# Less GpSimd work at the second norm, a sample step in full tiles, and another instruction order in a two-layer decoder step

## The chip, the cores and the metric

The kernel runs on one core of a Trainium2 chip. The metric is the device time of one execution in microseconds (us), as the median of several runs. The engines are named as the profile names them: PE is TensorE (matmuls), PEld its weight loads, DVE is VectorE, ACT is ScalarE, POOL is GpSimd, and SP (SyncE) issues most of the DMAs. "PEclk" in the profile is the granted clock of TensorE as a share of full speed.

## The reference

The program is one inference step of a hybrid decoder with two layers. There are T = 1032 token columns: 1024 of a prompt and 8 of a sample, one new token for each of 8 sequences with 8192 cached positions. Each layer computes:

```python
h = rmsnorm(x, g_norm1) * (1 + scale1) + shift1
proj = h @ w_in                                   # z, xbc, dt, cq, ckv, kpe, u
ssd  = ssd_mixer(...)       # Mamba-2: 6 heads x 64, state 128, 2 groups; prompt by chunks,
                            # sample by one step from state_ssm
mla  = attend(...)          # latent attention; the sample reads 64 pages of 128 positions a sequence
pool = pool_mixer(...)      # trailing means
mix  = concatenate([ssd, mla, pool]) @ w_out
x  = x + gate1 * mix
h2 = rmsnorm(x, g_norm2) * (1 + scale2) + shift2
x  = x + gate2 * ((silu(h2 @ w_gate) * (h2 @ w_up)) @ w_down)
```

The step of the sample in the SSD mixer is, for each sequence b and head h, state = exp(dt a) state + B (dt x)^T, then y = C . state + D x.

## The kernel before, in words

Columns are tokens, partitions are features. A product of fp32 values is made of three matmuls: every operand is cut into a high part (an ACT copy to fp32r, L88) and a low part (a subtraction, L89, on DVE or POOL as a constant says), and `mm3` (L133 to L135) issues high x high, low x high, high x low. The token columns of the FFN and of the output projection are cut into four quarters of 258 columns; a half `g` holds two.

A layer goes through these stages (in layer 0, us of the span): the input projection (to about 310); the **weave** (about 320 to 1030), in which `Weave` advances three generators in turn: `sample` (the pages of the sample's attention; `L1140`, `L1141` cut a page, L133 to L135 with 390 columns make its keys, L1158 and L1305 their norms, and 32 softmax steps a layer follow), the chain `ssd_prompt`, `ssd_sample`, `ssd_finish`, `mla_prompt`, and blocks of the next adaLN table; then the output projection `out_proj` (about 1030 to 1122, half 0 then half 1, eight rows `m` of output each); the second norm with the first FFN passes (1122 to about 1200); the other FFN passes; and the down projection. Layer 1 repeats it some 1800 us later.

One softmax step of `sample` is: L1190 makes `md` (DVE); L1195 multiplies it (one small matmul into `psm`); DVE subtracts at L1196; ACT takes the exponential at L1199 (`pb`); PE multiplies `pb` with the pages at L1205 (16 matmuls of 129 columns).

`ssd_sample` makes, for each of two groups g and two quarters q of the sequences, a new state `h` of 128 x 768 values: an outer product (L665, 8 partitions deep), a decay and an addition. `product` (L637 to L641) then multiplies it with C: 8 matmuls in pairs, each with a state tile as the weights (128 or 64 columns of it) and one moving column of C.

The second norm: `out_proj` makes the residual (L1411), its squares (ACT, L1417) and adds them over m (L1423, DVE for odd m, POOL for even m); `norm_half` sums over partitions by a matmul with ones (L1447), makes the reciprocal root `r` (L94 to L103), multiplies (`fresh`: L1457, then the scale on DVE, L1462, for k in `XFV` and on ACT, L1465, otherwise; L1469 and L1470 for the sample's columns) and builds the seven operands X of a Strassen product: `sub` (L1481) forms a sum, `cut` splits it into high and low, with POOL for the low part if the operand is in `XPL`. FFN pass n takes one of 22 blocks of columns of the weights through seven products (`PO`); the first two blocks are done for half 0 alone (passes 0 and 1), then for half 1 alone (passes 2 and 3), the other twenty for both. `up_conv` prepares the weights of a product: sums at L1538 (POOL if in `WPS` for the first blocks) and a cut (POOL if in `WPF`); `up_load` loads a block by two DMAs on SP. `up_first` loads the first block and prepares WAH = 3 products ahead. The FFN adds partial products at L1578 and multiplies gate and up at L1624.

The order of the instructions on each engine is not written out: a scheduler takes the program in its order as priority and decides by a simulation of the program which instruction comes next. Tiles of 128 x 1032 come from a pool of 24 buffers ("a") and of 128 x 1548 from one of 20 ("b").

Of the kernel before, what the change touches and what calls it, by code (L numbers as in the profile page):

```python
# [10 lines left out]
ALU = mybir.AluOpType  # L11
# [37 lines left out]
class Net:  # L49
# [385 lines left out]
    def softplus(self, l):  # L435
# [159 lines left out]
    def ssd_sample(self, l):  # L595
        nc, A = self.nc, self.A
        acr, ea = self.acr, self.ea
        x = [self.pj[6 + i] for i in range(3)]
        Bf = [self.pj[9 + i] for i in range(2)]
        Cf = [self.pj[11 + i] for i in range(2)]  # L600

        p = self.Gp()
        for h in range(6):
            nc.tensor.matmul(p[:, NB * h:NB * h + NB], self.K(K_ID + h, 1, r1=6).to_broadcast([6, 128]), ea,
                             start=True, stop=True)
        px = self.Gp()
        for i in range(3):
            for e in range(2):
                nc.tensor.matmul(px[64 * e:64 * e + 64, NB * i:NB * i + NB],
                                 self.K(K_ID + 64 + 2 * i + e, 1, 64, 70).to_broadcast([6, 64]), acr[64:70, TP:],  # L610
                                 start=True, stop=True)
        eb = self.S([128, 6, NB], "eb", bufs=1)
        nc.vector.tensor_copy(eb, p[:, 0:48].rearrange("p (h b) -> p h b", h=6))
        xd = self.S([128, 3, NB], "xd", bufs=1)
        for i in range(3):
            nc.vector.tensor_tensor(out=xd[:, i, :], in0=x[i][:, TP:], in1=px[:, NB * i:NB * i + NB],
                                    op=ALU.mult)
        yield 3
        p = self.Gp()
        for i in range(3):  # L620
            nc.tensor.transpose(p[0:NB, 128 * i:128 * i + 128], xd[:, i, :], self.K(K_ID, 128))
        xn = self.C(name="xnb")[0:NB, 0:384]
        nc.vector.tensor_copy(xn, p[0:NB, 0:384])
        p = self.Gp()
        for g in range(2):
            nc.tensor.transpose(p[0:NB, 128 * g:128 * g + 128], Bf[g][:, TP:], self.K(K_ID, 128))
        bn = self.C(name="bnb")[0:NB, 0:256]
        nc.vector.tensor_copy(bn, p[0:NB, 0:256])
        yield 3
        ysb = self.S([128, 24], "ysb", bufs=1)  # L630
        def product(g, q, h1):
            yp = self.Gp()
            for b in range(4):
                o = 192 * b
                cc = Cf[g][:, TP + 4 * q + b:TP + 4 * q + b + 1]
                if g == 0:
                    nc.tensor.matmul(yp[:, b:b + 1], h1[:, o:o + 128], cc, start=True, stop=True)  # L637
                    nc.tensor.matmul(yp[0:64, 4 + b:5 + b], h1[:, o + 128:o + 192], cc, start=True, stop=True)
                else:
                    nc.tensor.matmul(yp[64:128, b:b + 1], h1[:, o:o + 64], cc, start=True, stop=True)  # L640
                    nc.tensor.matmul(yp[:, 4 + b:5 + b], h1[:, o + 64:o + 192], cc, start=True, stop=True)  # L641
            for j, r, a in (((0, slice(0, 128), 0), (1, slice(0, 64), 4)) if g == 0 else
                            ((1, slice(64, 128), 0), (2, slice(0, 128), 4))):
                nc.vector.tensor_copy(ysb[r, 8 * j + 4 * q:8 * j + 4 * q + 4], yp[r, a:a + 4])

        pend = None
        def state(i):
            g, q = divmod(i, 2)
            h0[i] = self.C(name="h0")
            nc.sync.dma_start(h0[i][:, 0:768], A["sssm"][l, :, g, 4 * q:4 * q + 4, :].rearrange("n b e -> n (b e)"))  # L650
        h0 = {}
        state(0)
        for g in range(2):
            for q in range(2):

# [3 lines left out]
                nc.vector.tensor_tensor(  # L659
                    out=rhs[0:NB, 0:768].rearrange("p (b e) -> p b e", b=4),  # L660
                    in0=xn[:, 192 * g:192 * g + 192].unsqueeze(1).to_broadcast([NB, 4, 192]),
                    in1=self.K(K_ID + 4 * q, 4, r1=NB).unsqueeze(2).to_broadcast([NB, 4, 192]), op=ALU.mult)
                d = [self.Gp() for _ in range(2)]
                for a in range(2):
                    nc.tensor.matmul(d[a][:, 0:384], bn[:, 128 * g:128 * g + 128], rhs[0:NB, 384 * a:384 * a + 384],  # L665
                                     start=True, stop=True)
                for b in range(4):
                    (nc.gpsimd if PH else nc.vector).tensor_tensor(
                        out=h1[:, 192 * b:192 * b + 192].rearrange("p (h e) -> p h e", h=3),
                        in0=h0[2 * g + q][:, 192 * b:192 * b + 192].rearrange("p (h e) -> p h e", h=3),  # L670
                        in1=eb[:, 3 * g:3 * g + 3, 4 * q + b].unsqueeze(2).to_broadcast([128, 3, 64]), op=ALU.mult)
                del h0[2 * g + q]
                for a in range(2):
                    e = slice(384 * a, 384 * a + 384)
                    nc.vector.tensor_tensor(out=h1[:, e], in0=h1[:, e], in1=d[a][:, 0:384], op=ALU.add)
                nc.sync.dma_start(A["o_sssm"][l, :, g, 4 * q:4 * q + 4, :].rearrange("n b e -> n (b e)"), h1[:, 0:768])
                if pend is not None:
                    yield W_H
                    product(*pend)
                pend = g, q, h1  # L680
                yield
        yield 4
        product(*pend)
        yield
        for j in range(3):
            nc.vector.scalar_tensor_tensor(out=self.y[j][:, TP:], in0=x[j][:, TP:], scalar=self.V(l, V_DSK + j),
                                           in1=ysb[:, 8 * j:8 * j + 8], op0=ALU.mult, op1=ALU.add)

    def ssd_finish(self, l):
        nc = self.nc  # L690
# [680 lines left out]
    def out_proj(self, l, mod, xsrc, side):  # L1371
# [6 lines left out]
        for i, (g, m) in enumerate(todo):  # L1378
# [181 lines left out]
    def up_first(self, l):  # L1560

        self.passes = [(f, (g,)) for g in range(2) for f in range(NG0)] + [(f, (0, 1)) for f in range(NG0, FF)]
        self.wraw, self.wtmp, self.wop = {}, {}, {}
        self.nx = 0
        self.up_load(l, 0)
        for j in range(WAH):
            self.up_conv(l, j)

    def ffn(self, l, X, mod, side, sink):

# [9 lines left out]
        done = WAH + WA0  # L1580
        for j in range(7 * len(self.passes)):
            while done <= j + WAH:
                self.up_conv(l, done)
                done += 1
            n, i = divmod(j, 7)
            f, gs = self.passes[n]
            if j >= SD0 or gs != (0,):
# [119 lines left out]
def build(nc, tc, A):  # L1707
    with tc.tile_pool(name="c", bufs=1) as cp, tc.tile_pool(name="s", bufs=1) as sm, \
# [54 lines left out]
        for l in range(L):  # L1763
# [46 lines left out]
            for j in range(WA0):  # L1810
                n.up_conv(l, WAH + j)
            side = n.norm_half(1, mod, gs, 3, X)
            for _ in range(SD1):
                next(side)
# [170 lines left out]
def program(nc, arrays):  # L1985
# [25 lines left out]
```

## Time and profile before

| | before |
|---|---|
| median of 3 runs | 3662.61 us (3662.19 to 3663.1) |
| the profiled execution's own time | 3663.35 us |
| its span, first to last instruction | 3661.6 us |
| mean granted TensorE clock | 0.962 |
| busy in the span: PE, DVE | 3436.4 us, 2358.1 us |
| busy in the span: ACT, POOL | 1732.6 us, 1546.8 us |

The profiled execution is a run of its own beside the three; its time is 1.75 us above its span. Stages are given in us from the start of the span. A busy PE does not say that it works at full speed: PEclk has to be read with it.

### The profile page before, as it was taken

Reading aid. Unit: us, or ns where it says so; the run is one execution under the profiler, and the core shown is the slowest. Engines: PE = TensorE matmul, PEld = TensorE weight load, DVE = VectorE, ACT = ScalarE, POOL = GpSimd, SP = SyncE. Lnnn points to the kernel's source line nnn. Section 1 sums busy time; section 2 is a strip of 40 time slices with the busy share of each in tenths; the row PEclk is TensorE's granted clock in tenths of the full one; section 3 lists DMA queues with packets and bytes.
Section 4 is the critical chain, followed back from the end, with each engine's and each line's share of the span. In section 5 each row is a group of like instructions: output and inputs, shape, how many; then the busy total and the mean of one; then the engine's idle time right before and its main releaser. Section 6 shows DMA issues by size and latency. Waiting matters only on the chain. (4 is left out here: it accounts for less than half of the span.)

```text
span 3661.6 us, 66619 instructions
## 1 busy us (share of the span) xinstructions
PE 3436.4 (94%) x23740; PEld 3091.1 (84%) x23740; DVE 2358.1 (64%) x4308; ACT 1732.6 (47%) x4455; POOL 1546.8 (42%) x1173
## 2 busy tenths in 40 slices
PE   8988989899997999999999899998998979999999
PEld 6977767677787999999999776677777979999999
DVE  4568686778878555542345687777877685555433
ACT  4227466777844333331132365777776443333220
POOL 2225444444244655543222254445453455555431
PEclk9999799999998999999999998999999989999999
DMA  5234555544442222142222255554443522222432
GB/s 199 47 83 146 167 180 174 157 139 117 142 143 86 86 80 86 72 173 89 81 77 61 81 168 174 176 149 112 125 126 109 159 79 82 77 81 81 170 97 70
DMA packets 255322, 430.10 MB, mean 117 GB/s; under 512 B 38736, under 2 KB 180944, under 8 KB 254992
## 3 DMA queue, kind: packets, MB, share of 16 engines
q1 hardware_dynamic: 246800, 409.04, 35.2%
q0 software_dynamic: 8192, 16.79, 1.8%
q8 instruction: 190, 3.11, 0.4%
q14 instruction: 140, 1.15, 0.1%
HBM read 372.84 MB, written 52.87 MB: 116 GB/s over the span
## 5 line engine op out<-in xcount | busy, mean ns | idle before, releaser
L1158 ACT ACTIVATE sqk<-psd 128x384 f32<-128x384 f32 x1024 | 497.6, 503 | 234.2 <-PE psd L135 184.5
L1141 POOL TENSOR_TENSOR lt<-pg,lt 128x512 fp32r<-128x512 f32 x256 | 311.3, 1224 | 544.1 <-ACT lt L1140 426.5
L1305 DVE TENSOR_REDUCE ss<-sqk 128x12 f32<-128x768 f32 x448 | 421.3, 943 | 127.0 <-ACT sqk L1158 125.7
L133 PE MATMUL psd<-mv,lt 128*128 128x390 f32 x1024 | 439.8, 429 | 7.0 <-ACT scr L1159 6.9
L134 PE MATMUL psd<-X,wp 128*128 128x258 f32 x1408 | 400.9, 285 | 3.2 <-DVE wp L89 3.2
L133 PE MATMUL psd<-X,wp 128*128 128x258 f32 x1408 | 401.2, 285 | 0.0
L135 PE MATMUL psd<-X,wp 128*128 128x258 f32 x1408 | 400.8, 285 | 0.0
L134 PE MATMUL psd<-mv,lt 128*128 128x390 f32 x1024 | 369.6, 361 | 5.9 <-POOL lt L1141 5.9
L135 PE MATMUL psd<-mv,lt 128*128 128x390 f32 x1024 | 367.8, 359 | 0.0
L134 PE MATMUL psg<-X,wp 128*128 128x258 f32 x1056 | 302.9, 287 | 35.4 <-DVE wp L89 35.4
L135 PE MATMUL psg<-X,wp 128*128 128x258 f32 x1056 | 302.2, 286 | 0.0
L133 PE MATMUL psg<-X,wp 128*128 128x258 f32 x1056 | 301.8, 286 | 0.0
L1093 POOL DMA_INDIRECT kp<-kpeT,kidx x256 | 249.1, 973 | 124.2 <-issue 91.6
L133 PEld LDWEIGHTS psd<-mv,lt 128*128 128x128 f32 x1024 | 204.4, 200 | 105.4 <-issue 46.4
L89 POOL TENSOR_TENSOR wl<-wr,wh 128x1024 fp32r<-128x1024 f32 x47 | 125.7, 2679 | 374.5 <-ACT wh L88 288.3
L134 PEld LDWEIGHTS psd<-X,wp 128*128 128x128 f32 x1408 | 269.5, 191 | 3.5 <-DVE wp L89 3.5
L133 PEld LDWEIGHTS psd<-X,wp 128*128 128x128 f32 x1408 | 269.9, 192 | 0.0
L133 PE MATMUL psd<-op,wh 128*128 128x348 f32 (+1 forms) x792 | 252.6, 319 | 18.1 <-DVE pb L419 9.5
L135 PEld LDWEIGHTS psd<-X,wp 128*128 128x128 f32 x1408 | 269.6, 191 | 0.0
L134 PE MATMUL psd<-op,wl 128*128 128x348 f32 (+1 forms) x792 | 251.0, 317 | 10.5 <-DVE wl L89 5.7
L135 PE MATMUL psd<-op,wh 128*128 128x348 f32 (+1 forms) x792 | 249.8, 317 | 1.8 <-POOL op L89 1.4
L89 POOL TENSOR_TENSOR wp<-wr,wp 128x512 fp32r<-128x512 f32 x128 | 167.1, 1306 | 198.5 <-ACT wp L88 194.0
(466 smaller groups left out, 9898.6 us busy)
## 6 DMA issues: line engine op xcount, KB each, us to landing
pg<-pages SPq DMA_DIRECT2D x1024, 129.0 KB
wa<-wada SPq DMA_DIRECT2D x96, 512.0 KB
wr<-wff SPq DMA_DIRECT2D x96, 512.0 KB
ar<-actd SPq DMA_DIRECT2D x44, 516.0 KB
actd<-G SPq DMA_DIRECT2D x40, 516.0 KB
wd<-wdn SPq DMA_DIRECT2D x48, 384.0 KB
wr<-win SPq DMA_DIRECT2D x32, 512.0 KB
wr<-wout SPq DMA_DIRECT2D x32, 512.0 KB
```

The source lines that it names most:

```text
L89: (eng or nc.gpsimd).tensor_tensor(out=l, in0=x, in1=h.bitcast(F32), op=ALU.subtract)
L133: nc.tensor.matmul(ps, wh, xh, start=start, stop=False)
L134: nc.tensor.matmul(ps, wl, xh, start=False, stop=False)
L135: nc.tensor.matmul(ps, wh, xl, start=False, stop=stop)
L1093: self.nc.gpsimd.indirect_dma_start(out=kts[-1][:, 128 * g:128 * g + 128], out_offset=None, in_=self.A["kpeT"], in_offset=bass.IndirectOff ...
L1141: nc.gpsimd.tensor_tensor(out=ll, in0=v, in1=lh.bitcast(F32), op=ALU.subtract)
L1158: nc.scalar.activation(out=sq, in_=d[:, kc], func=AF.Square)
L1305: nc.vector.tensor_reduce(out=o, in_=x, axis=AX.X, op=ALU.add)
```

## The change

It has three parts. (1) `TileContext` is opened with `schedule_with_timeline_sim=True`, so that the scheduler decides by its timeline simulation. (2) In `ssd_sample`, tiles of 6 or 8 partitions are now tiles of 128 with zeros around the values; `product` now takes a tile `zc` (C of eight sequences, one column every 129, zeros elsewhere) as the weights and the state as 192 moving columns: four matmuls that add up into one bank, where row b of the result is sequence b; three transposes at the end turn the result back. (3) Around the second norm the constants `XPL`, `XFV`, `WPF`, `WPS` are emptied: the low parts of X and of the first weights and the first weights' sums go from POOL to DVE, and the scale of k = 1, 3 from DVE to ACT. `OPV` names the weights of `out_proj` whose low part DVE makes: 9, 11, 13, 15 are added. The sum of squares of half 1 is all on DVE. `up_first` goes from after half 0 of `out_proj` to its row m = 3, and two weights each are prepared at m = 4 to 7, so that eight are ready ahead where three were.

```diff
--- before.py
+++ after.py
...
-        ea = self.ea = self.S([6, NB], "ea", bufs=1)
-        nc.scalar.activation(out=ea, in_=p[0:6, 128 - NB:128], func=AF.Exp)
+        ea = self.ea = self.S([128, NB], "ea", bufs=1)
+        nc.gpsimd.memset(ea, 0.0)
+        nc.scalar.activation(out=ea[0:6], in_=p[0:6, 128 - NB:128], func=AF.Exp)
...
+        t = self.C(name="xnb")
+        xn, bn, xd = t[:, 0:384], t[:, 384:640], t[:, 640:1024].rearrange("p (i x) -> p i x", i=3)
+        nc.gpsimd.memset(xd, 0.0)
...
+        zs = [self.C(name="zc") for _ in range(2)]
+        for z, cf in zip(zs, Cf):
+            nc.gpsimd.memset(z, 0.0)
+            nc.vector.tensor_copy(z[:, 0:129 * NB].rearrange("p (b x) -> p b x", x=129)[:, :, 0], cf[:, TP:])
         yield 3
...
         def product(g, q, h1):
             yp = self.Gp()
-            for b in range(4):
-                o = 192 * b
-                cc = Cf[g][:, TP + 4 * q + b:TP + 4 * q + b + 1]
-                if g == 0:
-                    nc.tensor.matmul(yp[:, b:b + 1], h1[:, o:o + 128], cc, start=True, stop=True)
-                    nc.tensor.matmul(yp[0:64, 4 + b:5 + b], h1[:, o + 128:o + 192], cc, start=True, stop=True)
...
-                nc.vector.tensor_copy(ysb[r, 8 * j + 4 * q:8 * j + 4 * q + 4], yp[r, a:a + 4])
+            for b in range(4 * q, 4 * q + 4):
+                o = 192 * (b - 4 * q)
+                nc.tensor.matmul(yp[:, 0:192], zs[g][:, 128 * b:128 * b + 128], h1[:, o:o + 192], start=b == 4 * q,
+                                 stop=b == 4 * q + 3)
...
                 for a in range(2):
-                    nc.tensor.matmul(d[a][:, 0:384], bn[:, 128 * g:128 * g + 128], rhs[0:NB, 384 * a:384 * a + 384],
+                    nc.tensor.matmul(d[a][:, 0:384], bn[:, 128 * g:128 * g + 128], rhs[:, 384 * a:384 * a + 384],
                                      start=True, stop=True)
...
+        p = self.Gp()
+        for j in range(3):
+            nc.tensor.transpose(p[:, 128 * j:128 * j + 128], yb[:, 128 * j:128 * j + 128], self.K(K_ID, 128))
...
                 for _ in range(SDO):
                     next(side[0], None)
+            elif m == UF0:
+                self.up_first(l)
+            elif m > UF0:
+                for _ in range(UFN):
+                    self.up_ahead(l)
...
-                (nc.vector if m % 2 else nc.gpsimd).tensor_tensor(out=sqs[z], in0=sqs[z], in1=sq, op=ALU.add)
+                (nc.vector if g or m % 2 else nc.gpsimd).tensor_tensor(out=sqs[z], in0=sqs[z], in1=sq, op=ALU.add)
...
-        for j in range(WAH):
-            self.up_conv(l, j)
+        self.done = 0
+
+    def up_ahead(self, l):
+        self.up_conv(l, self.done)
+        self.done += 1
...
-            n.up_first(l)
             side[0] = n.norm_half(0, mod, gs, 3, X)
...
-WPT, WPL, XPT, XPL, GUP = (0, 1, 2, 3), (0, 2, 4, 6), (), (1, 5, 7), 0
+WPT, WPL, XPT, XPL, GUP = (0, 1, 2, 3), (0, 2, 4, 6), (), (), 0
...
+UF0, UFN = 3, 2
 WA0, W_L, W_F, W_G = 0, 10, 28, 5
 OPO = (6, 7, 0, 1, 2, 3, 4, 5)
-XFV, WPF, WPS, OPV = (1, 3), (2,), (0, 1), (0, 2, 4, 6, 8, 10, 12, 14)
+XFV, WPF, WPS, OPV = (), (), (), (0, 2, 4, 6, 8, 9, 10, 11, 12, 13, 14, 15)
...
-    with tile.TileContext(nc) as tc:
+    with tile.TileContext(nc, schedule_with_timeline_sim=True) as tc:
```

In the order of PE's instructions, the first fences show a softmax step of layer 0 (names: `md` is what L1190 made, `pb` the exponentials, `psm` the bank; L1195 of before is L1204 of after, L1205 is L1214). Before:

```order
L1195 MATMUL psm_2986<-md_2923,kt 128x6
L135 MATMUL psd_2992<-mv_1410,lt_2886 128x390
L133 MATMUL psd_3009<-mv_1410,lt_2886 128x390
L134 MATMUL psd_3009<-mv_1410,lt_2886 128x390
L510 MATMUL psg_2975<-acr_1626,kt 128x128 x3
L510 MATMUL psg_2998<-acr_1626,kt 128x128 x3
L135 MATMUL psd_3009<-mv_1410,lt_2886 128x390
...
L573 MATMUL psg_3055<-M_2802,xn_2961 64x128
L575 MATMUL psg_3055<-E_2803,st_2251 64x128
L1205 MATMUL psm_3068<-pg_2211,pb_190 32x129 x4
```

After:

```order
L1204 MATMUL psm_2987<-md_2924,kt 128x6
L544 MATMUL psg_3153<-cv_1738,cv_1391 128x128
L544 MATMUL psg_3153<-cv_1877,cv_1573 128x128
L556 MATMUL psg_3166<-kt,cv_1027 128x128
L556 MATMUL psg_3166<-kt,cv_1128 128x128
L556 MATMUL psg_3166<-kt,cv_1229 128x128
L1214 MATMUL psm_3069<-pg_2212,pb_190 32x129 x4
```

Before, 21 rows of other work (seven matmuls of 390 columns and 18 of 128) stand between the small matmul and the one that needs its exponentials; after, five matmuls of 128 columns do. Over the 64 steps of the program the columns between the two have a median of 4530 before and of 2720 after. For L828 to L853 of `mla_prompt` it is the other way, 12,700 and 22,400.

The next fences show PE in `ssd_sample` of layer 0 (`h` is a state, `cv` holds C, `hr` is the outer product's right side, `psg_3916` and `psg_3924` are the product's banks). Before:

```order
L665 MATMUL psg_3874<-hr_3868,bnb_3781 128x384
L637 MATMUL psg_3916<-cv_1737,h_579_3838 128x1
L638 MATMUL psg_3916<-cv_1737,h_579_3838 64x1
L133 MATMUL psd_3990<-mv_1410,lt_3858 128x390
L134 MATMUL psd_3990<-mv_1410,lt_3858 128x390
```

After:

```order
L671 MATMUL psg_3882<-hr_3876,xnb_3715 128x384
L133 MATMUL psd_4004<-mv_1410,lt_3866 128x390
L134 MATMUL psd_4004<-mv_1410,lt_3866 128x390
L135 MATMUL psd_4004<-mv_1410,lt_3866 128x390
L642 MATMUL psg_3924<-h_578_3846,zc_3723 128x192 x4
```

The pair L637, L638 stands four times before (once shown); in its place four matmuls of 192 columns follow each other. One such group stands in each layer for each g and q.

The last fences show DVE in the second norm of half 1 in layer 0 (`xb` is the residual, `r` the reciprocal root, `wp` a prepared weight, `G` and `s` FFN sums; L1457 of before is L1471 of after, L1578 is L1595). Before:

```order
L103 SCALAR_TENSOR_TENSOR r_13551<-rw_13553,r_13551 128x258
L1457 TENSOR_TENSOR xb_12941<-xb_12941,r_13551 128x1032
L1457 TENSOR_TENSOR xb_12942<-xb_12942,r_13551 128x1032
L1462 TENSOR_SCALAR xb_12941<-xb_12941,gs_12918,mod_76 128x258 x2
L1462 TENSOR_SCALAR xb_12942<-xb_12942,gs_12918,mod_76 128x250 x2
L1469 TENSOR_TENSOR xb_12942<-xb_12942,gs_12918 128x4x8
L89 TENSOR_TENSOR wp_13603<-wt_12925,wp_13603 128x512
```

After:

```order
L103 SCALAR_TENSOR_TENSOR r_13565<-rw_13567,r_13565 128x258
L1595 TENSOR_TENSOR s_13615<-s_13615,psg_13673 128x258
L1595 TENSOR_TENSOR G_13613<-G_13613,psg_13658 128x258
L1471 TENSOR_TENSOR xb_12956<-xb_12956,r_13565 128x1032
L1471 TENSOR_TENSOR xb_12954<-xb_12954,r_13565 128x1032
L89 TENSOR_TENSOR wp_13688<-wr_12741,wp_13688 128x512
```

Before, the first weight `wp` that DVE cuts in this place stands behind the whole normalization; after, FFN sums (L1595) stand between its parts, since eight weights are already prepared, and no L1462 is left on DVE. From the first L94 of half 1 to the fourth L1639 (L1624 of before) DVE's order of after holds 36 instructions of 258 columns, 30 of 512, 15 of 1032, 4 of 516 and 6 small ones. On SP, the four loads of the first two FFN blocks (`wr` from `wff`) stand between the sixth and the ninth load of `out_proj`'s weights; before, the first pair stood behind the tenth and the second pair behind the last of them.

## Rows read from the trace of the kernel before

**Rows 1.** The page: the span, and busy time of each engine.

```profile
span 3661.6 us, 66619 instructions
PE 3436.4 (94%) x23740; PEld 3091.1 (84%) x23740; DVE 2358.1 (64%) x4308; ACT 1732.6 (47%) x4455; POOL 1546.8 (42%) x1173
```

**Rows 2.** Windows: length, busy time of each engine, PEclk, DMA share, GB/s.

```profile
core 0: us, PE busy (x) PEld busy (x) DVE busy (x) ACT busy (x) POOL busy (x), PEclk, DMA share, GB/s
372.00:432.00 60.00, 58.07 (x299) 44.88 (x298) 33.59 (x76) 22.55 (x74) 25.16 (x31) 0.72 0.61 194
432.00:1020.00 588.00, 541.29 (x3486) 423.44 (x3485) 461.45 (x846) 423.84 (x1332) 257.66 (x232) 0.96 0.49 146
1030.00:1080.00 50.00, 49.65 (x402) 48.90 (x402) 31.84 (x48) 20.17 (x38) 19.61 (x12) 1.00 0.52 170
1080.00:1120.00 40.00, 35.78 (x271) 35.37 (x272) 35.62 (x46) 18.48 (x31) 20.82 (x9) 0.91 0.46 145
1120.00:1190.00 70.00, 50.65 (x341) 49.40 (x340) 64.56 (x92) 35.45 (x65) 27.70 (x14) 0.80 0.23 76
2186.00:2254.00 68.00, 64.57 (x344) 50.42 (x342) 41.68 (x97) 27.74 (x94) 27.04 (x33) 0.77 0.56 181
2254.00:2820.00 566.00, 522.73 (x3371) 413.90 (x3371) 448.59 (x821) 417.93 (x1313) 255.16 (x228) 0.96 0.47 136
2920.00:2990.00 70.00, 50.74 (x342) 49.48 (x342) 62.81 (x89) 34.74 (x62) 27.92 (x15) 0.80 0.23 78
```

**Rows 3.** Waits of PE: who ended them, us in total, times, longest.

```profile
PE psg L134 <- DVE wp L89: 35.4, 7, 8.6
PE psg L853 <- DVE rx L839: 12.2, 4, 3.2
PE psm L1205 <- ACT pb L1199: 11.7, 7, 3.2
PE psm L1195 <- DVE md L1190: 11.3, 12, 2.5
```

**Rows 4.** A fine window of PE in the sample's step: busy, PEclk, DMA share, GB/s.

```profile
398.00:402.00 4.00, 4.00 (x10) 0.50 0.00 0
```

**Rows 5.** PE's timeline in layer 0: start, us, instruction.

```profile
334.81 0.81 PE L583 MATMUL psg<-xn 128*128 128x192 f32 x4
...
411.86 0.28 PE L640 MATMUL psg<-cv,h 128*64 128x1 f32 x2
...
412.38 0.28 PE L640 MATMUL psg<-cv,h 128*64 128x1 f32 x2
```

**Rows 6.** One softmax step on the timelines of PE and ACT.

```profile
327.66 0.28 PE L1195 MATMUL psm<-md,kt 128*128 128x6 f32 x2
```
```profile
331.26 0.32 ACT L1199 ACTIVATE pb<-scr 128x96 f32<-128x96 f32 x1
```

**Rows 7.** PE's timeline at the second norm of half 1, layer 0.

```profile
1122.06 0.59 PE L1447 MATMUL psd<-sq,kt 128*128 128x258 f32 x2
...
1137.96 0.58 PE L134 MATMUL psg<-X,wp 128*128 128x258 f32 x1 [8.60 <-DVE wp L89]
```

**Rows 8.** DVE's timeline at the same place, and the end of pass 3.

```profile
1131.82 5.38 DVE L1462 TENSOR_SCALAR xb<-xb,gs,mod 128x258 f32<-128x258 f32 x4
...
1140.01 1.22 DVE L89 TENSOR_TENSOR X<-xb,X 128x1032 fp32r<-128x1032 f32 x1
...
1142.36 0.41 DVE L1578 TENSOR_TENSOR G<-G,psg 128x258 f32<-128x258 f32 x1
1142.69 0.68 DVE L89 TENSOR_TENSOR wp<-wr,wp 128x512 fp32r<-128x512 f32 x1
1143.30 0.41 DVE L1578 TENSOR_TENSOR s<-s,psg 128x258 f32<-128x258 f32 x1
...
1195.68 1.35 DVE L1624 TENSOR_TENSOR G<-G,U 128x516 f32<-128x516 f32 x1 [0.41 <-ACT G L1623]
```

**Rows 9.** POOL: its timeline beside rows 8, and its memsets of 1032 columns.

```profile
1130.50 3.62 POOL L89 TENSOR_TENSOR X<-xb,X 128x1032 fp32r<-128x1032 f32 x1 [11.37 <-ACT X L88]
```
```profile
L471 POOL MEMSET acr<- 128x1032 f32 x2 | 1.9, 974 | 0.0
```

More of the change, by code (lines that the diff above doesn't have):

```diff
@@ L603, in ssd_sample @@
         for h in range(6):
-            nc.tensor.matmul(p[:, NB * h:NB * h + NB], self.K(K_ID + h, 1, r1=6).to_broadcast([6, 128]), ea,
+            nc.tensor.matmul(p[:, NB * h:NB * h + NB], self.K(K_ID + h, 1).to_broadcast([128, 128]), ea,
                              start=True, stop=True)
         px = self.Gp()
[L607 to L611, printed above, removed]
+        for h in range(6):
+            nc.tensor.matmul(px[:, NB * h:NB * h + NB], self.K(K_ID + 64 + h, 1).to_broadcast([128, 128]), acr[:, TP:],
+                             start=True, stop=True)
         eb = self.S([128, 6, NB], "eb", bufs=1)
         nc.vector.tensor_copy(eb, p[:, 0:48].rearrange("p (h b) -> p h b", h=6))
[L614 to L617, printed above, removed]
+        t = self.C(name="xnb")
+        xn, bn, xd = t[:, 0:384], t[:, 384:640], t[:, 640:1024].rearrange("p (i x) -> p i x", i=3)
+        nc.gpsimd.memset(xd, 0.0)
+        for h in range(6):
+            r = slice(64 * (h % 2), 64 * (h % 2) + 64)
+            nc.vector.tensor_tensor(out=xd[r, h // 2, 128 - NB:], in0=x[h // 2][r, TP:],
+                                    in1=px[r, NB * h:NB * h + NB], op=ALU.mult)
+        zs = [self.C(name="zc") for _ in range(2)]
+        for z, cf in zip(zs, Cf):
+            nc.gpsimd.memset(z, 0.0)
+            nc.vector.tensor_copy(z[:, 0:129 * NB].rearrange("p (b x) -> p b x", x=129)[:, :, 0], cf[:, TP:])
         yield 3
@@ L620, in ssd_sample @@
         for i in range(3):
-            nc.tensor.transpose(p[0:NB, 128 * i:128 * i + 128], xd[:, i, :], self.K(K_ID, 128))
-        xn = self.C(name="xnb")[0:NB, 0:384]
-        nc.vector.tensor_copy(xn, p[0:NB, 0:384])
+            nc.tensor.transpose(p[:, 128 * i:128 * i + 128], xd[:, i, :], self.K(K_ID, 128))
+        nc.vector.tensor_copy(xn, p[:, 0:384])
         p = self.Gp()
         for g in range(2):
-            nc.tensor.transpose(p[0:NB, 128 * g:128 * g + 128], Bf[g][:, TP:], self.K(K_ID, 128))
-        bn = self.C(name="bnb")[0:NB, 0:256]
-        nc.vector.tensor_copy(bn, p[0:NB, 0:256])
+            nc.tensor.transpose(p[:, 128 * g:128 * g + 128], Bf[g][:, T - 128:], self.K(K_ID, 128))
+        nc.vector.tensor_copy(bn, p[:, 0:256])
         yield 3
-        ysb = self.S([128, 24], "ysb", bufs=1)
+        yb = xd.rearrange("p i x -> p (i x)")
         def product(g, q, h1):
             yp = self.Gp()
-            for b in range(4):
-                o = 192 * b
-                cc = Cf[g][:, TP + 4 * q + b:TP + 4 * q + b + 1]
-                if g == 0:
-                    nc.tensor.matmul(yp[:, b:b + 1], h1[:, o:o + 128], cc, start=True, stop=True)
-                    nc.tensor.matmul(yp[0:64, 4 + b:5 + b], h1[:, o + 128:o + 192], cc, start=True, stop=True)
[L639 to L643, printed above, removed]
-                nc.vector.tensor_copy(ysb[r, 8 * j + 4 * q:8 * j + 4 * q + 4], yp[r, a:a + 4])
+            for b in range(4 * q, 4 * q + 4):
+                o = 192 * (b - 4 * q)
+                nc.tensor.matmul(yp[:, 0:192], zs[g][:, 128 * b:128 * b + 128], h1[:, o:o + 192], start=b == 4 * q,
+                                 stop=b == 4 * q + 3)
+            o = yb[:, 192 * g:192 * g + 192]
+            if q:
+                nc.vector.tensor_tensor(out=o, in0=o, in1=yp[:, 0:192], op=ALU.add)
+                zs[g] = None
+            else:
+                nc.vector.tensor_copy(o, yp[:, 0:192])
         pend = None
@@ L659, in ssd_sample @@
                 nc.vector.tensor_tensor(
-                    out=rhs[0:NB, 0:768].rearrange("p (b e) -> p b e", b=4),
-                    in0=xn[:, 192 * g:192 * g + 192].unsqueeze(1).to_broadcast([NB, 4, 192]),
-                    in1=self.K(K_ID + 4 * q, 4, r1=NB).unsqueeze(2).to_broadcast([NB, 4, 192]), op=ALU.mult)
+                    out=rhs[:, 0:768].rearrange("p (b e) -> p b e", b=4),
+                    in0=xn[:, 192 * g:192 * g + 192].unsqueeze(1).to_broadcast([128, 4, 192]),
+                    in1=self.K(K_ID + 128 - NB + 4 * q, 4).unsqueeze(2).to_broadcast([128, 4, 192]), op=ALU.mult)
                 d = [self.Gp() for _ in range(2)]
                 for a in range(2):
-                    nc.tensor.matmul(d[a][:, 0:384], bn[:, 128 * g:128 * g + 128], rhs[0:NB, 384 * a:384 * a + 384],
+                    nc.tensor.matmul(d[a][:, 0:384], bn[:, 128 * g:128 * g + 128], rhs[:, 384 * a:384 * a + 384],
                                      start=True, stop=True)
@@ L684, in ssd_sample @@
         yield
+        p = self.Gp()
+        for j in range(3):
+            nc.tensor.transpose(p[:, 128 * j:128 * j + 128], yb[:, 128 * j:128 * j + 128], self.K(K_ID, 128))
         for j in range(3):
             nc.vector.scalar_tensor_tensor(out=self.y[j][:, TP:], in0=x[j][:, TP:], scalar=self.V(l, V_DSK + j),
-                                           in1=ysb[:, 8 * j:8 * j + 8], op0=ALU.mult, op1=ALU.add)
+                                           in1=p[:, 128 * j:128 * j + NB], op0=ALU.mult, op1=ALU.add)
     def ssd_finish(self, l):
@@ L1579, in ffn @@
         last = self.passes[-1][0]
-        done = WAH + WA0
         for j in range(7 * len(self.passes)):
-            while done <= j + WAH:
-                self.up_conv(l, done)
-                done += 1
+            while self.done <= j + WAH:
+                self.up_ahead(l)
             n, i = divmod(j, 7)
@@ L1809, in build @@
                 pass
-            for j in range(WA0):
-                n.up_conv(l, WAH + j)
+            for _ in range(WA0):
+                n.up_ahead(l)
             side = n.norm_half(1, mod, gs, 3, X)
```

## The prediction

> **What bounds the kernel now.** I read the page first. PE is busy 3436.4 of 3661.6 us, DVE 2358.1 [rows 1]. So time can be saved in three ways only: less idle time of PE, fewer matmuls, or a higher granted clock under matmuls that stay. The windows come next, because the mean of 94% hides where these are [rows 2]. In the stretch 1030 to 1080 PE is busy 49.65 of 50 us at PEclk 1.00: nothing to gain there. Three stretches of each layer differ. The stretch around the sample's SSD step (372 to 432, 2186 to 2254) has a busy PE, 58.07 of 60 and 64.57 of 68, but at 0.72 and 0.77 of full speed. The rest of the weave (432 to 1020, 2254 to 2820) has PE idle for 46.7 and 43.3 us at 0.96. The second norm (1120 to 1190, 2920 to 2990) has PE busy 50.65 and 50.74 of 70 at 0.80, while DVE is busy 64.56 and 62.81: here DVE is the bound. The list of PE's waits says the same by name: the largest is for `wp`, the low part of a weight made by DVE, 35.4 us in 7 waits, and the others are spread over the weave, 12.2, 11.7 and 11.3 us in a few waits each [rows 3]. The change touches all three stretches, so I cost them apart.
>
> **A, the sample's step in full tiles.** What PE does in 372 to 432 is worth 58.07 x 0.72 = 41.8 us at full clock. In the rest of the weave a microsecond carries 541.29 / 588 x 0.96 = 0.884 us of such work. At that rate the same work takes 47.3 us, 12.7 less. For layer 1: 64.57 x 0.77 = 49.7, at 522.73 / 566 x 0.96 = 0.887, gives 56.1, 11.9 less. Together -24.6. Whether the clock returns is a choice. For it: the stretch of slow clock coincides with the matmuls that fill a corner of the array, 8 rows deep or one column wide, and these are what the change replaces. In a piece of it PE is busy 4.00 of 4.00 us and the clock stays at 0.50 [rows 4], which is the lower of the two levels, so being busy did not bring it back; what the change alters is how full the work is. Bounds: nothing at all, or the whole loss 0.28 x 60 + 0.23 x 68 = 32.4 us.
>
> The page "TensorE: Matmul & The Clock Gate" of the Trainium skill, section "What's actually happening", says that the clock is set by how busy PE has been recently. The 4.00 us just read do not fit with busy time as the measure; if the rule held in that form, filling the tiles would return nothing.
>
> The instructions themselves: a pair of one-column products takes 412.38 - 411.86 = 0.52 us [rows 5], four pairs 2.08 for a g and q. Instead come four matmuls of 192 columns. They run as eight instructions, and four of that size take 0.81 us [rows 5], so 1.62 at most: -0.46, four times in each of two layers, -3.7. The three transposes at the end, six instructions of 128 columns, cost below the 0.81 x 6 / 4 x 128 / 192 = 0.8 us of that row, two layers 1.6; I take 1.0. Net -2.7. The outer product of 128 rows instead of 8 has the same columns, so I charge PE nothing. POOL gets three memsets a layer, two of 1032 columns at 974 ns [rows 9] and a smaller one, 2.5 us where it is busy 25.16 of 60 [rows 2]; a `yield` of the generator lies between them and their use. Without that cover they would cost 5 us in all. A = -24.6 - 2.7 = **-27.3**.
>
> **B, the second norm.** From the first matmul with ones to the end of pass 3 the program now takes 1195.68 - 1122.06 = 73.6 us [rows 7, 8]. The 8.60 us wait ends when DVE has made a weight, behind four L1462 that took 5.38 us [rows 8]; one such instruction alone takes about the 0.41 of other 258-column operations. During those four POOL ran its low part of X, 3.62 us [rows 9], and both seem to be held up. Without POOL I price DVE by the rows of 258, 512 and 1032 columns: 0.41, 0.68 and 1.22 us each, or by distance of starts 0.33 (1142.36 to 1142.69) and 0.61 (1142.69 to 1143.30) [rows 8]. The order gives 36, 30, 15, 4 of 516 columns and 6 small ones. By duration: 14.8 + 20.4 + 18.3 + 4 x 1.35 + 1 = 59.9 us. By distance, with 0.68 for 516 columns: 11.9 + 18.3 + 18.3 + 2.7 + 1 = 52.2. These instructions are queued back to back, so I take 54, near the lower end, and 3 us from the first matmul to DVE's first instruction: 57 instead of 73.6, -16.6 a layer. The upper end gives -10.6. Is DVE still what is late? PE's work there is 50.65 x 0.80 = 40.5 us at full clock in the 70 [rows 2], below 54, so yes, DVE stays the bound. ACT gets eight scales more a half and has 35.45 of 70 busy; its cover is large; uncovered they would cost 3.3 us a half at the 0.41 us that such an operation takes on DVE.
>
> What DVE takes over earlier lies in `out_proj`. In half 0 it is busy 31.84 of 50 [rows 2]; eight prepared weights at 0.68 and their sums add about 9 us, hidden. In half 1 it is busy 35.62 of 40 already, with PE idle 4.2 and 0.09 x 40 = 3.6 us lost by the clock. There three low parts of X (3.7), four of weights of 1024 columns (4.9 at the price of 1032) and four sums of squares (2.7) come to it, 11.3 us; some of the scales, the first weights' preparation and the time lost beside POOL leave. I take half of the 7.8 us as won, -4 a layer, with a loss of 4 as the other bound. The two loads that `up_first` issues, and the next two, pass in front of two and three loads of `out_proj` weights on SP. The DMA share there is 0.52, so I charge nothing; if each of the four delayed PE by a transfer of 512 KB at 170 GB/s, 3 us, it would be 12 us a layer. B = 2 x (-16.6 - 4) = **-41.2**, bounds 2 x (-10.6 + 4) = -13 and, with the DMAs late as well, +11.
>
> **C, the order.** The trace of before cannot show what a new order does. A gain is bounded by the idle time of PE in the rest of the weave, 46.7 + 43.3 = 90 us [rows 2]. A loss: PE can wait for the exponentials after L1195 only as long as the chain takes. One chain runs from 327.94 to 331.58, 3.6 us [rows 6], and is covered by the matmuls placed between. Now the median cover shrinks by 4530 - 2720 = 1810 columns. `out_proj` at full clock puts 402 matmuls of 258 columns through in 49.65 us [rows 2], 2090 columns a microsecond, so the lost cover is 0.87 us; 64 steps make 55 us if none of it was slack. For `mla_prompt` the cover grows, and its waits were 12.2 us [rows 3]. I take **0**, since idle time of 8% leaves room for both signs.
>
> **The sum.** -27.3 - 41.2 + 0 = -68.5 against the profiled execution's own 3663.35 us: 3594.9. The median of the runs is 0.7 lower, so I forecast 3594.
>
> **The rivals.**
>
> R1, the clock does not come back in the sample's step: 3594 + 24.6 = 3619. For it: the weave around L665 mixes small matmuls of other generators in as well. Against it: the rest of the weave has them too and runs at 0.96 [rows 2].
>
> R2, the second norm stays as DVE-bound as it is: DVE takes 59.9 us, and half 1 of `out_proj` loses 4 us a layer. B is -13: 3594 + 28 = 3622. For it: 35.62 of 40 busy. Against it: the 5.38 us for four L1462, slowed beside POOL.
>
> R3, the order takes cover from the softmax steps: half to all of the 55 us is exposed, 40 as the middle: 3634. For it: the two PE fences of the change. Against it: 7 waits of 64 only, so that most steps had slack [rows 3].
>
> R4, the order fills half of PE's idle time: -45, so 3549. For it: waits of 12 us each on four lines show places with a bad order. Against it: cover at L1205 shrinks.
>
> R5, slower: every softmax step of the sample waits as long as the seven do that wait now, 11.7 / 7 = 1.67 us [rows 3]. 64 x 1.67 = 107: 3701. It decides from 76 us on (68.5 and the 7.3 of 0.2%), which is 1.19 us a step. A chain of 3.6 us with a cover of five matmuls of 128 columns could do it; against it speaks that other chains are much shorter, as only seven steps wait.
>
> R6, no change: the full tiles return no clock, DVE's new work eats what POOL's absence gives, and the order moves nothing that counts: about 3662.
>
> **How the numbers follow.** Chances: forecast 0.38, R1 0.13, R2 0.12, R3 0.12, R4 0.11, R5 0.09, R6 0.05. Range 3535 to 3650: it takes in R1 to R4 with the bounds of C around R3 and R4, and leaves R5 and R6 out with the tails. The likeliest case's own range is 3575 to 3610. Faster by over 0.2% (7.3 us, about what a measurement can tell): 0.86. Within: 0.05. Slower: 0.09.
>
> **What would show it.** A right: PEclk above 0.90 in the 60 us around L671 and L642; wrong: below 0.80. B right: from the first matmul with ones of half 1 to the fourth L1639 it takes 54 to 63 us, and PE's waits for DVE's `wp` fall from 35.4 us to below 15; wrong: DVE is busy all the time and the span stays near 73. In half 0 of `out_proj` PE stays at 49 of 50 us; a wait for `wh` there would be the moved DMAs. C: PE's idle time outside these stretches, 90 us before, within 30 of that; waits of L1214 for `pb` above 40 us would be R3, above 75 R5. The prediction is wrong most likely where C is far from 0, since it rests on no row.

## The result and the profile after

The changed kernel takes 3742.32 us (3739.35 to 3750.76, 4 runs) against 3662.4 for before: ratio 1.0222, interval 1.0204 to 1.024. It is 80 us slower where 68.5 us less were forecast. Its profiled execution has a span of 3737.5 us at a mean granted clock of 0.956. The page's busy times, beside [rows 1]:

```profile
span 3737.5 us, 66458 instructions
PE 3460.0 (93%) x23682; PEld 3102.1 (83%) x23682; DVE 2359.4 (63%) x4328; ACT 1741.4 (47%) x4487; POOL 1450.8 (39%) x1131
```

PE is busy 23.6 us longer with fewer instructions, at a mean granted clock of 0.956 against 0.962, and it is idle 277.5 us instead of 225.2. The windows of the stages, moved with the stages (sample's step, rest of the weave, second norm, then layer 1), answer to [rows 2]:

```profile
core 0: us, PE busy (x) PEld busy (x) DVE busy (x) ACT busy (x) POOL busy (x), PEclk, DMA share, GB/s
389.00:449.00 60.00, 50.27 (x298) 38.85 (x297) 47.92 (x92) 26.48 (x87) 30.52 (x38) 0.91 0.59 189
449.00:1059.00 610.00, 546.99 (x3434) 424.91 (x3433) 442.56 (x830) 416.11 (x1315) 249.54 (x227) 0.93 0.47 140
1167.00:1237.00 70.00, 59.77 (x426) 57.17 (x426) 61.04 (x99) 40.65 (x76) 11.31 (x8) 0.88 0.24 78
2235.00:2303.00 68.00, 58.90 (x334) 44.78 (x333) 50.82 (x99) 30.35 (x101) 36.11 (x43) 0.87 0.58 186
2303.00:2901.00 598.00, 530.54 (x3336) 415.69 (x3335) 437.49 (x819) 410.79 (x1302) 246.71 (x222) 0.94 0.44 128
3010.00:3080.00 70.00, 60.00 (x427) 57.18 (x426) 60.56 (x97) 40.65 (x76) 10.60 (x7) 0.88 0.23 75
```

In the sample's step the clock rose from 0.72 to 0.91, but PE is idle 9.7 of 60 us where it was 1.9, and DVE is busy 47.92 where it was 33.59. The second norm holds 426 matmuls in 70 us where it held 341. The rest of the weave takes 610 and 598 us where 588 and 566 did, and PE idles 63.0 and 67.5 us of it at a lower clock. The list of PE's waits, against [rows 3]:

```profile
PE psg L886 <- DVE mt L889: 30.0, 23, 5.0
PE psg L862 <- DVE rx L848: 25.3, 6, 5.2
PE psd L133 <- DVE pj L285: 14.7, 5, 6.4
PE psm L1214 <- ACT pb L1208: 12.9, 14, 1.5
...
PE psg L642 <- DVE h L681: 7.1, 2, 3.9
...
PE psg L671 <- DVE h L681: 6.0, 2, 3.0
```

The 35.4 us for `wp` are gone from the top. In their place stand waits of the prompt's attention for DVE (L886 of after is L877 of before, 30.0 us where it was 3.1; L862 is L853), waits for the evacuations of the input projection (L285, 14.7 us where it was 1.2), and waits for the state in the sample's step.

### The profile page after: what moved, and what is told of

It is laid out like the page before. It is cut to its first block, busy times and chain, and to the rows that moved or that the text cites. A ratio compares the mean times of both kernels' runs of the same rounds, so it can differ in the third digit from the quotient of the medians.

```text
span 3737.5 us, 66458 instructions
## 1 busy us (share of the span) xinstructions
PE 3460.0 (93%) x23682; PEld 3102.1 (83%) x23682; DVE 2359.4 (63%) x4328; ACT 1741.4 (47%) x4487; POOL 1450.8 (39%) x1131
## 5 line engine op out<-in xcount | busy, mean ns | idle before, releaser
L133 PE MATMUL psd<-mv,lt 128*128 128x390 f32 x1024 | 413.5, 404 | 5.0 <-ACT scr L1168 3.7
L133 PE MATMUL psd<-X,wp 128*128 128x258 f32 x1408 | 401.9, 286 | 9.6 <-ACT wp L88 9.4
L135 PE MATMUL psd<-X,wp 128*128 128x258 f32 x1408 | 398.8, 284 | 0.0
L134 PE MATMUL psd<-mv,lt 128*128 128x390 f32 x1024 | 362.7, 354 | 0.0
L135 PE MATMUL psd<-mv,lt 128*128 128x390 f32 x1024 | 359.0, 351 | 0.0
L133 PE MATMUL psg<-X,wp 128*128 128x258 f32 x1056 | 301.9, 286 | 8.6 <-ACT wp L88 8.6
L135 PE MATMUL psg<-X,wp 128*128 128x258 f32 x1056 | 300.8, 285 | 0.0
L133 PE MATMUL psd<-op,wh 128*128 128x348 f32 (+1 forms) x792 | 254.6, 324 | 35.0 <-DVE pj L285 14.7
L133 PEld LDWEIGHTS psd<-X,wp 128*128 128x128 f32 x1408 | 268.4, 191 | 11.9 <-ACT wp L88 11.8
L135 PEld LDWEIGHTS psd<-X,wp 128*128 128x128 f32 x1408 | 268.0, 190 | 0.0
L133 PEld LDWEIGHTS psd<-mv,lt 128*128 128x128 f32 x1024 | 200.8, 196 | 80.1 <-issue 28.3
L89 POOL TENSOR_TENSOR wl<-wr,wh 128x1024 fp32r<-128x1024 f32 x39 | 101.6, 2610 | 392.7 <-ACT wh L88 275.5
L135 PE MATMUL psd<-op,wh 128*128 128x348 f32 (+1 forms) x792 | 250.5, 318 | 1.7 <-POOL op L89 1.5
L135 PE MATMUL psd<-ac,wh 128*128 128x344 f32 x704 | 225.0, 322 | 6.6 <-DVE ac L89 5.0
```

What stands on the lines that cost most here:

```text
L89: (eng or nc.gpsimd).tensor_tensor(out=l, in0=x, in1=h.bitcast(F32), op=ALU.subtract)
L133: nc.tensor.matmul(ps, wh, xh, start=start, stop=False)
L134: nc.tensor.matmul(ps, wl, xh, start=False, stop=False)
L135: nc.tensor.matmul(ps, wh, xl, start=False, stop=stop)
```

## The experiments

**The three parts apart.** Edits: the order alone,

```diff
-    with tile.TileContext(nc) as tc:
+    with tile.TileContext(nc, schedule_with_timeline_sim=True) as tc:
```

everything but this line; part (2) of the change alone; part (3) alone.

> Before with nothing changed but the scheduler's timeline simulation. Theory 1 (the new order costs, the rest gains): slower than before by 70 to 130 us, 3735 to 3790; the input projection and the weave are longer in both layers by some 15 to 30 us each, as in the changed kernel, and the second norm is as before. Theory 2 (the order is about neutral, and the loss comes from the work that moved to DVE and from the waits for DVE in the sample's step): within 20 us of 3662. Theory 3 (the order helps and the other parts lose even more): below 3642.

> The changed kernel without the timeline simulation. Theory 1: faster than before by 30 to 70 us, 3590 to 3632, with PEclk near 1.0 around the sample's SSD step and 4 to 12 us less a layer from the start of the second norm to the end of the FFN. Theory 2: 3720 to 3760, slower than before by as much as the changed kernel. Theory 3: above 3762.

> Before with the sample's SSD step in full tiles and nothing else. Theory 1: the clock comes back, PEclk above 0.9 in the 60 us of that step, 12 to 28 us faster in all, 3634 to 3650. Theory 2: the waits of PE for the state (L681, 14 us in the changed kernel) are the price of the step itself, so within 5 us of before or slower, though the clock is back.

> Before with only the part around the second norm: no POOL work there, the first weights prepared during the output projection. Theory 1: 41 us faster by the forecast, about 3621, if the stretch from the first matmul with ones of half 1 to the end of pass 3 falls from 73.6 to 57 us and the output projection does not grow. Theory 2: the output projection grows by 4 to 12 us a layer (in the changed kernel the time from the last page to the first matmul with ones of half 0 is 49 us where it was 42), so that at most 15 us are left: 3647 to 3665.

| | median us | ratio to before, interval |
|---|---|---|
| order alone | 3738.71 | 1.0212, 1.0193 to 1.023 |
| all but the order | 3638.11 | 0.9935, 0.9918 to 0.9952 |
| sample's step alone | 3647.07 | 0.9955, 0.9941 to 0.9969 |
| second norm alone | 3650.49 | 0.9968, 0.9952 to 0.9985 |

(Before took 3663.08 us here.) Theory 1 holds in kind: the order costs 76 us by itself, and the rest gains 25; alone the step gains 16 and the norm 13. The gains are smaller than theory 1 had them: 30 to 70 were expected of the rest and 41 of the norm, whose 13 are what theory 2 of that run allows, at most 15. On top of the order the rest gains nothing: 3742 with it, 3739 without.

The trace of the order alone has PE busy 3477.0 us, 40.6 more for the same 23740 instructions, and idle 257.0, 31.8 more. By stage, it is 20 us late at the first page product (L1205) of layer 0 (352.2 against 332.1), 39 at the last (1061.8 against 1022.7), 45 at the first matmul of the down projection; in layer 1 it is 53 us late at the first page product (2200.5 against 2147.7) and 74 at the last (2895.9 against 2821.8). FFN and down projections lose nothing. So 28 of the 72 us are lost ahead of the two weaves, where the input projection's evacuations stand (L285: PE waits 16.0 us for them in the whole program, 1.2 before); no experiment below takes that stage by itself. A piece of the weave shows the pattern; PE's timeline of the kernel with the order alone:

```profile
602.27 0.33 PE L877 MATMUL psg<-ah,ah 128*128 128x128 f32 x1
602.44 0.27 PE L879 MATMUL psg<-fr 128*128 128x128 f32 x1
603.90 0.49 PE L877 MATMUL psg<-ah,ah 128*128 128x512 f32 x1 [1.19 <-DVE mt L880]
605.23 0.58 PE L877 MATMUL psg<-ah,ah 128*128 128x256 f32 x1 [0.84 <-DVE mt L880]
605.61 0.31 PE L879 MATMUL psg<-fr 128*128 128x128 f32 x1
606.45 0.80 PE L877 MATMUL psg<-ah,ah 128*128 128x512 f32 x1 [0.53 <-DVE mt L880]
607.18 1.95 PE L1205 MATMUL psm<-pg,pb 128*32 128x129 f32 x32
609.06 0.69 PE L133 MATMUL psd<-mv,lt 128*128 128x390 f32 x1
609.55 0.53 PE L134 MATMUL psd<-mv,lt 128*128 128x390 f32 x1
...
611.78 0.34 PE L135 MATMUL psd<-mv,lt 128*128 128x390 f32 x1
```

and DVE's beside it:

```profile
603.17 0.68 DVE L880 TENSOR_REDUCE mt<-psg 128x1 f32<-128x512 f32 x1
603.77 0.81 DVE L1280 TENSOR_TENSOR mv<-qabs,mv 128x6 fp32r<-128x6 f32 x1
604.50 0.67 DVE L880 TENSOR_REDUCE mt<-psg 128x1 f32<-128x512 f32 x1
605.10 0.93 DVE L1305 TENSOR_REDUCE ss<-sqk 128x12 f32<-128x768 f32 x1
605.96 0.23 DVE L1196 TENSOR_TENSOR scr<-scr,psm 128x96 f32<-128x96 f32 x1
606.12 0.27 DVE L880 TENSOR_REDUCE mt<-psg 128x1 f32<-128x128 f32 x1
```

Four L877 stand next to each other with no keys (L133 to L135) between; there are three banks (`psg`) for their results, and DVE empties one only between other work. PE waits 2.56 us; the granted clock is 0.99 from 600 to 605 us and 0.52 from 605 to 612; and the same 390-column matmul takes 0.53 us and later 0.34. Here the waits are paid a second time in clock.

How much of the 40.6 us more of busy time is clock can be estimated. In the clock records of the two traces PE is busy 229.7 us at the lower level before and 282.2 with the order. At that level the starts of these matmuls lie 0.33 us apart (609.87 and 610.20), later, at full clock, 0.18 (612.42 and 612.60). So about half of the 52.5 us more, some 26, is what the clock costs; the other 15 are not accounted for.

**Are these bank waits the price?** Every second row block of that loop takes its banks from the other pool, with the order and, as a control, without:

```diff
-                p = self.Gp()
+                p = self.Dp() if i % 2 else self.Gp()
                 nc.tensor.matmul(p[:, 0:b - a], qh[:, n - 128:n], kh[:, a:b], start=True, stop=b != n)
```

> The timeline order on the kernel before, with seven instead of three PSUM banks for the first loop of the prompt's attention (every second row block takes its banks from the other pool). Theory A (PE waits for banks that DVE has not emptied, and what follows at half clock, is what the order costs in the weave): PE's waits of L877 for mt fall from 32.6 to below 12 us, and the time falls by 25 to 45 us from the 3739 of the order alone, to 3694 to 3714. Theory B (these waits are only where a chain that is late anyway shows itself, and PE will wait at the next place): the waits fall, the time stays within 10 us of 3739.

> The same seven banks in the kernel before, without the timeline order, as the control. It waited 3.1 us there only, so both theories expect 3655 to 3670. If it gains as much as the timeline order does from the banks, the banks help for another reason than those waits.

With the order 3755.28 us (1.026, 1.0236 to 1.0284), without it 3670.78 (1.0022, 1.0012 to 1.0031), so the edit costs 9 us by itself. With the order neither theory has this time: A expected 25 to 45 us less than 3739, B the same. PE's wait with the order alone:

```profile
PE psg L877 <- DVE mt L880: 32.6, 26, 6.6
```

and with the order and the edit:

```profile
PE psm L1205 <- ACT pb L1199: 29.6, 25, 3.9
...
PE psd L133 <- DVE mt L880: 22.4, 12, 4.6
...
PE psd L877 <- DVE mt L880: 13.0, 4, 6.2
```

L877 waits 16.1 us (13.0 for the other pool's banks and 3.1 for its own) instead of 32.6, but the keys, whose banks it now shares, wait 22.4 for the same reduction, 38.5 in sum, and the softmax steps 29.6 instead of 19.6. Banks shared with the keys do not cure the order; the wait moves. Since the waits for this reduction did not go away, the run does not say what the time would be without them: that they are the price is neither shown nor refuted.

**Does the loss need this program order?** The generators' own waits are left out of the weave, with and without the timeline order:

```diff
-                        e[0] = self.now + (next(e[1]) or 1)
+                        next(e[1])
+                        e[0] = self.now + 1
```

> Before, with the waits that the generators hand to the weave left out: each generator gets its turn in every round, so the program is written in a cruder interleaving. Without the timeline order. It should be slower than before, by 20 to 150 us; it is the base of the next run.

> The same cruder interleaving with the timeline order. Theory A (the timeline order loses because it leaves an interleaving that was laid out for this chip): what it costs here is below half of the 76 us, or it gains. Theory B (its order is worse by itself, whatever order the program is written in): it costs 55 to 95 us here as well.

3863.1 us (1.0546, 1.0528 to 1.0563) without, 3930.6 (1.0738, 1.072 to 1.0756) with: the order costs 67.5 us on a program that is 201 us slower (20 to 150 were expected). That is theory B's time. The loss does not need the waits that were set by hand; the rest of the program's order stayed as it was.

**Which engine's order?** One engine is held to program order for the whole program (here DVE; `Activation` in the second pair), again with and without the timeline order:

```diff
-        build(nc, tc, A)
+        with tc.manual_schedule(engines={mybir.EngineType.DVE}):
+            build(nc, tc, A)
```

> Before, with DVE issuing its instructions in the order in which the program is written; the other engines are left to the scheduler, without the timeline order. It is the base of the next run; since DVE can no longer take what is ready first, slower than before by 0 to 150 us.

> The same with the timeline order for the other engines. Theory A (the loss sits in DVE's new order: evacuations and softmax steps behind work that nobody waits for): less than 25 us above the run before it. Theory B (the loss sits in PE's own new order, which comes to its operands too early): 50 to 100 us above it.

> Before, with ACT issuing in the order in which the program is written, without the timeline order: the base of the next run, slower than before by 0 to 100 us.

> The same with the timeline order for the other engines. Theory A (DVE's order) and theory B (PE's order) both expect 50 to 100 us above the run before it; less than 25 us would say that it is ACT's new order that costs.

DVE held: 3941.86 (1.0764, 1.0746 to 1.0782) and 4023.74 (1.0989, 1.097 to 1.1007), +81.9. ACT held: 3788.66 (1.035, 1.0333 to 1.0367) and 3855.81 (1.0536, 1.0519 to 1.0554), +67.2. In the first pair DVE's instructions stand in the same order in both programs, in the second ACT's do. The loss stays, so neither engine's new order is needed for a loss of this size, though on programs that are 280 and 127 us slower than before (at most 150 and 100 were expected). PE's own order is a candidate that is left, and theory B's; the same test on PE was not run, and POOL's and SP's orders were free in both pairs. Against SP speaks that PE waits for transfers hardly longer with the order alone, 8.9 us against 7.2. Which engine's order carries the loss stays open.

**The product alone.** Before with the new `product`, the two `zc` tiles and the three transposes; the outer product keeps its 8 rows.

> Before with the product of state and C in full tiles alone; the outer product stays 8 rows deep. Theory A (the one-column products let the clock fall): PEclk above 0.9 in the step and as fast as the whole step in full tiles, 3642 to 3652. Theory B (the outer products of 8 rows do): PEclk stays below 0.8 and the time within 6 us of before. Theory C (DVE's work in the step takes what the clock gives): the clock is back but the time is within 6 us of before.

3663.97 us (0.9999, 0.9989 to 1.0008): no change. Two windows in the step, layer 0 and 1, before:

```profile
400.00:420.00 20.00, 20.00 (x104) 16.54 (x103) 8.67 (x19) 5.89 (x21) 11.02 (x14) 0.59 0.47 138
2210.00:2230.00 20.00, 20.00 (x99) 16.04 (x98) 9.01 (x21) 4.98 (x19) 8.98 (x12) 0.59 0.37 112
```

and with the product alone:

```profile
400.00:420.00 20.00, 19.17 (x119) 15.74 (x118) 16.28 (x32) 10.43 (x34) 16.07 (x19) 0.94 0.72 209
2210.00:2230.00 20.00, 19.62 (x128) 16.12 (x126) 17.41 (x36) 9.88 (x34) 16.02 (x19) 1.00 0.78 229
```

The clock is back with the product alone, so the one-column products went with the slow clock and not the 8-row outer product. And the time does not fall: PE is busy 3421.5 us in place of 3436.4, and idle 18 us more. DVE is at 16 to 17 of 20 us in these windows where it was at 9, and PE's waits for DVE in the softmax (`mx`, 11.6 us before) and for `rx` (12.2) grew by 21 us in sum, behind the step:

```profile
PE psm L1192 <- DVE mx L1187: 26.2, 7, 5.9
PE psg L859 <- DVE rx L845: 18.7, 6, 3.2
```

These are theory C's numbers, but its reason, DVE's work in the step, is not shown. The whole step alone has DVE as busy in these windows:

```profile
400.00:420.00 20.00, 18.02 (x120) 15.12 (x119) 18.05 (x33) 9.92 (x36) 16.40 (x18) 1.00 0.82 240
2210.00:2230.00 20.00, 18.14 (x118) 14.86 (x116) 17.27 (x33) 11.13 (x32) 9.78 (x10) 1.00 0.92 292
```

and it gains 16 us, with the waits for `mx` and `rx` at 11.6 and 12.2 as before. Why they grow with the product alone stays open.

**When the first weights are prepared.** First `up_first` and its three weights go back behind half 0 of `out_proj`, the rest of part (3) stays; then only the first block's loads are early:

```diff
-            elif m == UF0:
-                self.up_first(l)
-            elif m > UF0:
-                for _ in range(UFN):
-                    self.up_ahead(l)
...
+            n.up_first(l)
+            for _ in range(WAH):
+                n.up_ahead(l)
             side[0] = n.norm_half(0, mod, gs, 3, X)
```

> The part around the second norm alone (3650 in the run before), but with the first weights prepared at the old place, three ahead. Theory A (the early loads and copies make the output projection's weights late, 4 to 7 us a layer in its second half): the waits for wh fall from 15.7 us to below 8, the second half of the output projection is back at about 59 us, and since the weights of the first pass are now late again, 5 to 15 us a layer are lost behind it: 3640 to 3665. Theory B (the work that came to DVE and ACT makes it longer, wherever the first weights are prepared): the second half stays at 63 to 66 us and the first passes are longer than in the run before, 3655 to 3680.

> The part around the second norm alone, with only the two loads of the first block at the early place and the weights prepared at the old one. Theory A (the early preparation costs because up to thirteen of the 24 tiles are held by weights that wait for their use, so that the output projection's loads wait for a tile): with two tiles held, within 5 us of 3637, the time with everything at the old place. Theory B (the four loads of 512 KB take the DMA queues from the output projection's own loads): two of the four stay early, so half of the 13.6 us, about 3643 to 3650.

At the old place 3636.85 us (0.9924, 0.9908 to 0.9941), with the loads early 3627.6 (0.9907, 0.9887 to 0.9927), against 3650.49 with all early. The first run bears out theory A: PE's waits for `wh` fall from 15.7 us to 6.6, and in layer 0 the time from the last page product to the first matmul with ones of half 1 is 95.7 us (1021.2 to 1116.86) and 108.9 with all early (1021.7 to 1130.60). What is lost behind it is a little less than the 5 to 15 us that it said: 63.3 us to the fourth multiply against 59.2. So the constants alone gain 25 us, and preparing eight weights early gives back 13.6. In 1080 to 1100 PE is busy 16.85 of 20 us early, and 19.25 late:

```profile
1080.00:1100.00 20.00, 16.85 (x134) 16.02 (x133) 15.21 (x22) 14.55 (x25) 0.00 (x0) 1.00 0.34 111
```
```profile
1080.00:1100.00 20.00, 19.25 (x148) 19.04 (x148) 16.46 (x26) 15.41 (x28) 0.00 (x0) 0.91 0.62 186
```

Early, SP waits 12.4 us to load `xt` (L1404) in the output projection of layer 0, for DVE to be done with something that holds the tile, where it waits 3.3 with the weights at the old place:

```profile
SPq L1404 <- DVE wl L89: 5.1, 1, 5.1
SPq L1404 <- DVE xb L1421: 4.6, 1, 4.6
SPq L1404 <- DVE rv L94: 2.7, 1, 2.7
```

Two of the four loads early cost nothing, the time even falls below the 3632 to 3642 that theory A had, which speaks against the DMA queues; the other two were not tried. That the held tiles are the reason, and not the copies on ACT and DVE, fits these waits but is not shown.

**The parts that gain, together.** All of the change but the order and the early preparation:

> The changed kernel without the timeline order and with the first weights prepared at the old place: full tiles in the sample's step and the new constants. If the parts add up (16 us of the step, 25 us of the constants in the runs before): 3618 to 3630, faster than both kernels. If the gain of one hides in the other's: 3632 to 3640.

3621.89 us, ratio 0.9889 (0.9872 to 0.9905): 40 us faster than before and 120 faster than the change. The parts add up (16 + 25).

## Why the prediction was wrong

**C failed, and decided the sign.** The step was "I take 0, since idle time of 8% leaves room for both signs". Measured by itself it is +76 us; on the rest of the change +104 (3742.3 against 3638.1), so the sum also failed in adding C and the rest as if they did not meet. The prediction had named C as its weakest term, since no row stood behind it. The bound of a loss, 55 us, was too low in kind: it counted only the cover of the softmax steps, and no stage ahead of the weaves, where 28 us went. The softmax steps' waits for `pb` stayed near 12 us (11.7, now 12.9; 19.6 with the order alone), far below R3's 40, so R3 and R5 had the sign but not the place. I had counted the median cover, and L877 shows why that misleads: by the order, the columns from one L877 to the third after it have a median of 6746 before and 6982 with the order, but the lowest twentieth falls from 4662 to 1414. And I priced waits as idle time alone: of the order's 72 us of span, 32 are idle and 41 are longer busy time of the same matmuls, an estimated 26 of them by the clock. That was nowhere in the bounds. Which of the new orders does it, and through which wait, stays open.

**A: mechanism right, size off.** The clock came back (0.72 to 0.91 and 0.77 to 0.87 in the change's two layers, the second short of the 0.90 that was to show it; 0.94 and 1.00 in the windows of the product alone), so R1 is out. The eight instructions of a product take from 405.34 to 406.50, 1.16 us, where I allowed 1.62:

```profile
405.34 1.46 PE L642 MATMUL psg<-h,zc 128*128 128x192 f32 x8
406.50 0.47 PE L133 MATMUL psd<-mv,lt 128*128 128x390 f32 x1
```

But the term -24.6 turned clock into time at the rate of the rest of the weave, as if no wait behind it would grow. The product alone has the clock and gains 0, as PE's waits grow by as much; the whole step gains 16 of 27.3.

The rule of the Trainium skill ("TensorE: Matmul & The Clock Gate", "What's actually happening"), in the form that the clock follows how busy PE was, does not fit here either: the product alone made PE less busy in these windows, 19.17 of 20 instead of 20.00, and the clock went from 0.59 to 0.94.

**B: the norm right, `out_proj` wrong.** From the first matmul with ones of half 1 to the fourth multiply takes 63.1 us in the change (1169.69 to 1232.79) and 58.9 without the order (1123.76 to 1182.63), where 57 was forecast, 54 to 63 was to show it right, and 73.6 was measured before. "-4 a layer" for `out_proj` was the step that failed: early preparation, which I let hide in half 0, lost 13.6 us over both layers. Its cover was counted in DVE's free time alone, and not in tiles, copies or what queues behind. With the old place the part gains 25, of a forecast 41.2.

## What to carry to other kernels

Time a scheduler's switch by itself before anything rides on it: the gains of the other edits can vanish under it. A median distance hid the tight places of this order, and a wait of TensorE is to be priced with the slow matmuls that follow it. A clock that comes back need not come back as time: look at the waits behind it. Work moved ahead into idle time of an engine can cost more than it gives; that it does so by the buffers it holds is a guess here.

## What the runs showed of the hardware beyond that

In two pairs of 20 us windows of the same step PE was busy 20.00 us at a granted clock of 0.59, and 19.17 and 19.62 us at 0.94 and 1.00. What differed was the shape of a few matmuls, one moving column against 192, and the work that came into the window behind them.
